# Loading the norm weights inside the first chunk of x, and warming the matrix engine with 44 matmuls instead of 28

## The chip, the core and the metric

The kernel runs on one core of a Trainium2 chip. The metric is the device time of one execution in microseconds (us); lower is better. Three executions of the kernel before took 485.05, 485.16 and 486.32 us, so the median is 485.16 us. The engines that appear below are PE (TensorE: matmuls; PEld is its weight loading), DVE (VectorE), ACT (ScalarE), POOL (GpSimd) and SP, whose queue issues the kernel's DMAs.

## What is computed

A decoder layer with two attention branches (block-sparse "MoBA" and "NSA") over 512 tokens of width 1024. For the change only the first lines matter:

```python
def rms_norm(x, g):
    xf = x.astype(jnp.float32)
    y = xf * lax.rsqrt(jnp.mean(xf * xf, axis=-1, keepdims=True) + EPS)
    return (y * g.astype(jnp.float32)).astype(x.dtype)
...
h = rms_norm(x, norm_w[l])
proj = h @ w_in[l]
(q_a, k_a, v_a, z_a, q_b, kc, vc, ksl, vsl, kwn, vwn, gate_b, z_b, gate_m) = jnp.split(proj, split_points, axis=-1)
```

`x` is (1, 512, 1024) and `norm_w` has 1024 numbers. After it come the two attentions, their gates, two branch projections, the output projection and the addition of `x`.

## The kernel before, in words

The input is kept channel by token: `xT` is cut into eight chunks of 128 channels by 512 tokens, and chunk k is loaded into the tile `x` number k (one 256 KB DMA each). `norm_w` is laid out as 128 by 8, so that column k holds the weights of chunk k, and is loaded into the tile `w` (4 KB).

Every matmul is done in three parts to keep float32 accuracy: a value is split into a rounded part (`hh` of the input, `wh` of a weight tile) and the rest (`hl`, `wl`). `x_split` (L389) makes `hh` on ACT (L393, x times its weight column) and `hl` on DVE (L394). `x_square` (L400) squares each chunk on ACT (L406) and adds the squares up on DVE (L411) into `sq`. The factor 1/rms is not needed before the first projections: they run on the raw product, and `x_rms` (L425) sums `sq` over the channels with a few small matmuls (`pss`, L430), forms `rx` on DVE (L433) and POOL (L434, a power), and the results are scaled by `rx` when they leave PSUM.

The weights come as a stream of 256 KB tiles `wr`; four raw buffers exist (`NRAW`), so the fifth load waits until the first tile has been split. `wh` is made on ACT (L296) or POOL (L298), `wl` on DVE or POOL (L300). Two input chunks share one weight tile.

The first projection, `v0`, is `gemm_first` (L510): for each chunk k it issues twelve matmuls into four accumulators `pgf`, one for each 128 tokens, four with `hh` and `wh`, four with `hl` and `wh`, four with `hh` and `wl` (L523). So it can start as soon as chunk 0 and weight tile 0 have been split. The accumulators are read out (`v`, ACT L607 and DVE L608) once `rx` is known. The second projection, `qk0`, is `gemm_tok` (L497, matmuls at L325): four results `pgt` of 24 matmuls each; the first two use PSUM buffers of another ring, the third and fourth those that `v0` used, so that the third waits for the first `v`. After it come `pR` and `prx` (L627, L460), the next projections, and the transposes `pq` (L777) of the attention.

Before the first real matmul the kernel runs `NWARM` small matmuls of 128 columns on a zero tile (L386), which nobody reads.

The order of the instructions on every engine is worked out while the kernel is built: a planner keeps an estimated time for every engine and for the DMA queue (`dma`, L211, adds at least 450 ns for a load), and emits each step when its inputs should be ready. A change of one estimate thus can change the order elsewhere.

Of the kernel before, what the change touches and what calls it, by code (L numbers as in the profile page):

```python
# [12 lines left out]
F32 = mybir.dt.float32  # L13
F32R = mybir.dt.float32r
AF = mybir.ActivationFunctionType
ALU = mybir.AluOpType
AX = mybir.AxisListType

S = 512
D = 1024  # L20
DH = 64
P = 128
NT = S // P
KT = D // P
# [13 lines left out]
NGM = 5  # L38
NW = 8
NRAW = 4  # L40
NWARM = 28
LAT = 60
SHARE_A = 1.0
SHARE_F = 1.1
# [11 lines left out]
def tok_pieces():  # L56

    r = lambda a, n: list(range(a, a + n))
    d = {f"qk{p}": r(QA + 128 * p, 128) + r(KA_ + 128 * p, 128) for p in range(4)}
    d.update({f"v{i}": r(VA + 256 * i, 256) for i in range(2)})  # L60
    d.update({f"qb{i}": r(QB + 256 * i, 256) for i in range(2)})
    d["kb"] = r(KSL, 128) + r(KWN, 128) + r(GB, 24)
    d["vb"] = r(VSL, 128) + r(VWN, 128)
    return d


def chan_pieces():

    out = {"kc": KC, "vc": VC}
    for j in range(4):  # L70
        out[f"za{j}"] = ZA + 128 * j
        out[f"zb{j}"] = ZB + 128 * j
    for j in range(16):
        out[f"gm{j}"] = GM + 128 * j
    return out


def tok_layout():

    lay, n = {}, 0  # L80
    for name, cols in tok_pieces().items():
        lay[name] = (n, KT // 2, len(cols))
        n += KT // 2
    return lay, n


@with_exitstack
def hybrid_kernel(ctx: ExitStack, tc: tile.TileContext, x, xT, norm_w, wtok, wchan, gains, w1,
                  relone, wbr, wout, consts, out):
    nc = tc.nc  # L90
    cp = ctx.enter_context(tc.tile_pool(name="cp", bufs=1))
# [11 lines left out]
    def nm(s):  # L103
        uid[0] += 1
        return f"{s}{uid[0]}"
# [105 lines left out]
    def dma(dst, src, n, t=None):  # L211

        nc.sync.dma_start(out=dst, in_=src)
        free["Q"] = max(free["Q"], (now[0] if t is None else t) + 1000) + max(450, n * P / 360)
        return free["Q"] + 1000
# [127 lines left out]
    identr = cp.tile([P, P], F32R, name="identr")  # L343
    onesr = cp.tile([P, P], F32R, name="onesr")
    nc.vector.tensor_copy(onesr, ones.to_broadcast([P, P]))
    w8 = cp.tile([P, KT], F32, name="w8")
    rx = cp.tile([P, NT], F32, name="rx")
    nrx = cp.tile([P, NT], F32, name="nrx")
    R = cp.tile([P, S], F32, name="R")
    nc.scalar.activation(R[:, :8], mhalf, AF.Exp)  # L350
    kcs = cp.tile([P, 2, 2, C32], F32R, name="kcs")
    gate = cp.tile([P, 24, NT], F32, name="gate")
    cp.tile([P, 8], F32, name="pad")

    def cview(name):
        o, n = COFF[name]
# [15 lines left out]
    def att(name, dt=F32R):  # L372
        return ap_.tile([P, 512], dt, name=nm(name), tag="a")

    xts = [att("x", F32) for _ in range(KT)]
    xat = {}

    def load_x(k):
        xat[k] = dma(xts[k], xT[k * P:(k + 1) * P, :], 2048)

    now[0] = 700.0
    load_x(0)
    dma(w8, norm_w, 32)
    pw = pg.tile([P, 512], F32, name="pw", tag="g")
    for _ in range(NWARM):
        nc.tensor.matmul(pw[:, :P], warm[:, :1].to_broadcast([P, P]), warm[:, :1].to_broadcast([P, P]), start=True,  # L386
                         stop=True)

    def x_split(k):  # L389

        w = w8[:, k:k + 1]
        c = Chain(xat[k])
        c.do({"A": 613}, lambda e: e.activation(hh[:, k, :], xts[k], AF.Copy, scale=w)).mark(f"xh{k}")  # L393
        c.do({"d": 666}, lambda e: e.scalar_tensor_tensor(hl[:, k, :], xts[k], w, hh[:, k, :].bitcast(F32),  # L394
                                                          op0=ALU.mult, op1=ALU.subtract)).mark(f"xl{k}")

    sq_sum = att("sq", F32)
    sums = Chain(0.0)
# [66 lines left out]
    tlay, _ = tok_layout()  # L465
# [802 lines left out]
    for k in range(1, KT):  # L1268
        if k % 2:
            W.load()  # L1270
        load_x(k)
    W.load()
    W.bufs -= 1
    for k in range(KT):
        x_split(k)
        x_square(k)
# [30 lines left out]
def _consts():  # L1307
    i = np.arange(S)
    edges = np.array([16, 21, 27, 35, 46, 59, 77, 99, 128, 166, 216, 280, 363, 470])
    dist = S - 1 - i  # L1310
    bucket = np.where(dist < 16, dist, 16 + (dist[:, None] >= edges[None, 1:]).sum(1))
    onehot = (np.arange(32)[:, None] == bucket[None, :]).astype(np.float32)
    ident = np.eye(P, dtype=np.float32)
    ii = np.concatenate([np.eye(64, dtype=np.float32)] * 2, 0)
    t = np.arange(NT)[None, :] * P + np.arange(P)[:, None]
    c = np.arange(C32)
    cmask = np.where(16 * c[None, None, :] + 31 <= t[:, :, None], 0.0, NEG).astype(np.float32)
    rowv = (t >= 31).astype(np.float32)
    hmask = (np.arange(P)[:, None] // 64 == np.arange(2)[None, :]).astype(np.float32)
    return onehot, dict(ident=ident, ii=ii, cmask=cmask.reshape(P, -1), rowv=rowv, hmask=hmask)  # L1320


def _layout(inp):
    f = {k: np.asarray(v) for k, v in inp.items()}
    w_in = f["w_in"][0]
    lay, n = tok_layout()
    wtok = np.zeros((n, P, WT), np.float32)
    for name, cols in tok_pieces().items():
        i0, nt, m = lay[name]
        wtok[i0:i0 + nt, :, :2 * m] = w_in[:, cols].reshape(nt, 2, P, m).transpose(0, 2, 1, 3).reshape(nt, P, 2 * m)  # L1330
    ch = lambda w: w.reshape(-1, 4, P, P).transpose(0, 2, 1, 3).reshape(-1, P, 4 * P)
    wchan = np.stack([ch(w_in[:, c:c + P]) for c in chan_pieces().values()])
    gains = np.concatenate([f[k][0] for k in ("q_norm_a", "k_norm_a", "q_norm_b", "k_norm_cmp",
                                               "k_norm_sel", "k_norm_win")])
    posT = np.stack([f[k][0].reshape(16, 2, DH).transpose(1, 2, 0).reshape(P, 16)
                     for k in ("cmp_pos_k", "cmp_pos_v")], 1)
    w1 = np.stack([f[k][0].reshape(8, 2, P, CMPH).transpose(0, 2, 1, 3).reshape(8, P, 512)
                   for k in ("cmp_w1_k", "cmp_w1_v")])
    w2 = np.stack([f[k][0].reshape(2, P, DH).transpose(1, 0, 2) for k in ("cmp_w2_k", "cmp_w2_v")], 1)
    wbr = np.stack([np.concatenate([ch(f[k][0][:, j * P:(j + 1) * P]) for k in ("w_branch_a", "w_branch_b")], 0)  # L1340
                    for j in range(8)])
    wo = f["w_out"][0].reshape(4, 2, P, 4, 256).transpose(3, 0, 2, 1, 4).reshape(4, 4, P, 512)
    onehot, cd = _consts()
    cd.update(pos=posT.reshape(P, -1), w2=w2.reshape(P, -1))
    d = dict(x=f["x"][0], xT=f["x"][0].T, norm_w=f["norm_w"][0].reshape(KT, P).T, wtok=wtok, wchan=wchan, gains=gains, w1=w1,
             relone=np.tile(np.concatenate([f["rel_bias"], onehot], 1), (2, 1)), wbr=wbr, wout=wo,
             consts=np.concatenate([cd[k] for k in COFF], 1))
    return {k: np.ascontiguousarray(v) for k, v in d.items()}


_ORDER = ["x", "xT", "norm_w", "wtok", "wchan", "gains", "w1", "relone", "wbr", "wout", "consts"]


# [16 lines left out]
```

## Time and profile before

| | us |
|---|---|
| median of three executions | 485.16 |
| the profiled execution | 486.89 |
| its span, first to last instruction | 485.1 |
| PE busy in the span | 475.4 (98%) |
| DVE busy | 338.4 (70%) |
| ACT busy | 256.6 (53%) |
| POOL busy | 159.0 (33%) |

The profiled execution took 1.8 us more than its span, and 1.7 us more than the median of the three others. Times in rows are microseconds from the start of the span. The granted clock is given as a share of full speed; a matmul of 256 columns starts every 0.21 us at the lower of the engine's two clock levels (1.2 GHz) and every 0.12 us at the higher one (2.4 GHz), so that the spacing of matmuls tells the level too. A wait is put down to what ended it last.

### The profile page before, as it was taken

How to read it: one execution, taken by the hardware profiler on the slowest of the kernel's cores; microseconds unless marked ns; L12 is line 12 of the kernel's file. 1: busy time of each engine (PE TensorE's matmuls, PEld its weight loads, DVE VectorE, ACT ScalarE, POOL GpSimd, SP SyncE). 2: the span in 40 equal slices, each digit the busy share in tenths (PEclk: the TensorE clock that was granted, in tenths of full speed). 3: DMA queues.
4: the chain of work that ended last, by engine and by line, in shares of the span. 5: the costliest groups of instructions: out<-in, count | busy, mean ns of one | idle time of the engine just before them, and what ended most of it. 6: DMA issues, size and time to landing. Idle time of an engine off the chain costs nothing.

```text
span 485.1 us, 8685 instructions
## 1 busy us (share of the span) xinstructions
PE 475.4 (98%) x3060; PEld 426.7 (88%) x3060; DVE 338.4 (70%) x862; ACT 256.6 (53%) x631; POOL 159.0 (33%) x211
## 2 busy tenths in 40 slices
PE   7999999999999999999999999998999999999997
PEld 7999899999999989888888888886788888889997
DVE  5888999688898589797788677775555535444331
ACT  7656695477675286766686477764222231222210
POOL 0165577165555025465440254354000000000000
PEclk9999999999999999999999999998999999999999
DMA  8737243544344224122212221211133324526421
GB/s 275 221 74 171 61 134 112 151 114 135 79 123 140 74 66 113 41 65 68 65 45 75 84 68 57 49 42 45 43 106 112 94 81 139 166 76 217 142 89 43
DMA packets 28124, 49.15 MB, mean 101 GB/s; under 512 B 3313, under 2 KB 5745, under 8 KB 28081
## 3 DMA queue, kind: packets, MB, share of 16 engines
q1 hardware_dynamic: 28080, 48.60, 34.8%
q8 instruction: 24, 0.39, 0.4%
q14 instruction: 20, 0.16, 0.1%
HBM read 45.84 MB, written 2.75 MB: 100 GB/s over the span
## 4 chain that ended last, share of the span: by engine, by line
PE 95%; DVE 2%; DMA 1%; issue 0%; ACT 0%; POOL 0%; SPq 0%; DVEq 0%
PE pgc L325 30%; PE pgt L325 21%; PE po L325 9%; PE pbr L325 9%; PE O L926 6%; PE pt L892 6%; PE sps L845 3%; PE sps L846 3%; PE pgf L523 3%; PE pq L777 2%; PE hps L692 1%; DMA wr<-in_wtok 1%; PE hps L691 1%; PE scp L1014 1%; PE O L1070 0%
## 5 line engine op out<-in xcount | busy, mean ns | idle before, releaser
L300 DVE TENSOR_TENSOR wl<-wr,wh 128x512 fp32r<-128x512 f32 (+1 forms) x118 | 83.0, 712 | 7.3 <-ACT wh L296 7.0
L325 PE MATMUL pgc<-hh,wh 128*128 128x512 f32 x208 | 84.5, 406 | 0.0
L325 PE MATMUL pgt<-wh,hh 128*128 128x256 f32 (+1 forms) x288 | 82.6, 287 | 0.3 <-DVE v L608 0.3
L325 PE MATMUL pgc<-hh,wl 128*128 128x512 f32 x208 | 81.9, 394 | 0.0
L325 PE MATMUL pgc<-hl,wh 128*128 128x512 f32 x208 | 81.8, 393 | 0.0
L325 PE MATMUL pgt<-wl,hh 128*128 128x256 f32 (+1 forms) x288 | 81.2, 282 | 0.0
L325 PE MATMUL pgt<-wh,hl 128*128 128x256 f32 (+1 forms) x288 | 81.0, 281 | 0.0
L296 ACT CAST wh<-wr 128x512 fp32r<-128x512 f32 (+1 forms) x90 | 54.0, 616 | 27.5 <-DMA wr<-in_wout 21.9
L883 POOL TENSOR_SCALAR P<-P,sst,gate 128x512 f32<-128x512 f32 (+3 forms) x56 | 40.5, 727 | 62.8 <-DVE sst L882 46.8
L298 POOL TENSOR_SCALAR wh<-wr 128x512 fp32r<-128x512 f32 (+1 forms) x34 | 23.3, 687 | 114.9 <-DMA wr<-in_wchan 70.3
L864 DVE CUSTOM_DVE_ANT_0 sb<-sps,T 128x512 f32<-128x512 f32 (+3 forms) x96 | 46.0, 484 | 17.7 <-PE sps L846 16.6
L325 PEld LDWEIGHTS pgt<-wh,hh 128*128 128x128 f32 x288 | 54.3, 188 | 1.2 <-DVE v L608 0.5
L325 PEld LDWEIGHTS pgt<-wh,hl 128*128 128x128 f32 x288 | 54.2, 188 | 0.3
L325 PEld LDWEIGHTS pgt<-wl,hh 128*128 128x128 f32 x288 | 54.3, 188 | 0.0
L879 ACT ACTIVATE P<-sb,sst 128x512 f32<-128x512 f32 (+3 forms) x88 | 50.9, 580 | 6.3 <-DVE sst L864 6.0
L904 ACT CAST ph<-pt 128x512 fp32r<-128x512 f32 (+2 forms) x72 | 33.5, 477 | 26.0 <-PE pt L892 25.3
L325 PEld LDWEIGHTS pgc<-hl,wh 128*128 128x128 f32 x208 | 39.1, 188 | 9.1
L325 PEld LDWEIGHTS pgc<-hh,wh 128*128 128x128 f32 x208 | 39.1, 188 | 6.8
L325 PEld LDWEIGHTS pgc<-hh,wl 128*128 128x128 f32 x208 | 39.2, 188 | 6.7
L892 PE MATMUL pt<-cst,P 128*128 128x128 f32 x232 | 41.8, 278 | 0.3 <-POOL P L883 0.3
L906 DVE TENSOR_TENSOR pl<-pt,ph 128x512 fp32r<-128x512 f32 (+2 forms) x72 | 38.5, 548 | 4.1 <-ACT ph L904 3.7
L370 POOL TENSOR_TENSOR nr<-nss,mhalf 128x4 f32<-128x4 f32 x28 | 32.3, 1157 | 21.4 <-DVE nss L369 19.4
(208 smaller groups left out, 1076.6 us busy)
## 6 DMA issues: line engine op xcount, KB each, us to landing
wr<-in_wchan SPq DMA_DIRECT2D x52, 256.0 KB, 2.7
wr<-in_wtok SPq DMA_DIRECT2D x36, 256.0 KB, 2.8
T<-rtab SPq DMA_DIRECT2D x16, 256.0 KB, 3.8
wr<-in_w SPq DMA_DIRECT2D x16, 256.0 KB, 2.7
wr<-in_wbr SPq DMA_DIRECT2D x16, 256.0 KB, 2.6
wr<-in_wout SPq DMA_DIRECT2D x16, 256.0 KB, 2.9
x<-in_xT SPq DMA_DIRECT2D x8, 256.0 KB, 5.2
xr<-in_x SPq DMA_DIRECT2D x8, 256.0 KB, 4.4
```

Of the source, the lines that this page charges most:

```text
L296: e.copy(hi, raw)
L298: e.tensor_scalar(hi, raw, 1.0, 1.0, op0=ALU.mult, op1=ALU.mult)
L300: c.do(either(n), lambda e, hi=hi, lo=lo, raw=raw: e.tensor_sub(lo, raw, hi.bitcast(F32))).mark((w, 1, i))
L325: nc.tensor.matmul(dst, sts[i][a], mvs[i][b], start=(start and i == a == b == 0), stop=(stop and i == n - 1 and b == 1))
L370: c.do({"p": 430 + 150 * w}, lambda e: e.tensor_tensor(v(dst), v(ss), mhalf[:parts, :w], op=ALU.pow))
L864: e.tensor_tensor_reduce(z["sb"][:, :L], sps[:, :L], T[:, S - L:], scale=-1.0, scalar=3e38, op0=ALU.add, op1=ALU.min, accum_out=st[:, 0, b ...
L879: e.activation(pv(), z["sb"][:, :L], AF.Exp, bias=st[:, 0, b:b + 1], scale=-1.0, accum_out=st[:, 1, b:b + 1])
L883: c.do({"P": 315 + 0.834 * L}, lambda e: e.tensor_scalar(pv(), pv(), st[:, 2, b:b + 1], g, op0=ALU.mult, op1=ALU.mult))
L892: nc.tensor.transpose(pt[:, (b - kb) * P:(b - kb + 1) * P], u.p0 if u.p0 is not None and b == 0 else u.pb[:, POFF[b] + kb * P:POFF[b] + (k ...
L904: e.copy(z["w"][0], pt[:, :w])
L906: ch.do({"D": cd(w)}, lambda e: e.tensor_sub(z["w"][1], pt[:, :w], z["w"][0].bitcast(F32)), pt)
L926: nc.tensor.matmul(O[0][:, S - n:], v.bitcast(F32) if kb == 3 else v, w, start=(u.first and kb == 0 and i == 0), stop=(u.last and kb == 3 ...
```

## The change

`norm_w` is no longer an input of its own. On the host its 128 by 8 layout is put beside the first chunk of x, as columns 512 to 519 of a new input `x0` of 128 by 520. One DMA of 2080 B in each partition loads both into a tile `first`. That tile is taken from the ring `P` (two buffers, otherwise used by the attention and by `bias_rows`) and is given back when the last `hl` is done. The tile `w`, a 4 KB DMA and its place in SP's queue go away. `NWARM` becomes 44.

```diff
-NWARM = 28
+NWARM = 44
...
-    w8 = cp.tile([P, KT], F32, name="w8")
...
-    cp.tile([P, 8], F32, name="pad")
...
-    xts = [att("x", F32) for _ in range(KT)]
+    first = alloc("P", "x0", (P, 1280))
+    w8 = first[:, S:S + KT]
+    xts = [first[:, :S]] + [att("x", F32) for _ in range(1, KT)]
...
-        xat[k] = dma(xts[k], xT[k * P:(k + 1) * P, :], 2048)
+        xat[k] = dma(xts[k], xT[(k - 1) * P:k * P, :], 2048)
...
-    load_x(0)
-    dma(w8, norm_w, 32)
+    xat[0] = dma(first[:, :S + KT], x0, 2080)
...
                                                           op0=ALU.mult, op1=ALU.subtract)).mark(f"xl{k}")
+             first if k == KT - 1 else None).mark(f"xl{k}")
...
-    d = dict(x=f["x"][0], xT=f["x"][0].T, norm_w=f["norm_w"][0].reshape(KT, P).T, ...
+    d = dict(x=f["x"][0], xT=f["x"][0].T[P:],
+             x0=np.concatenate([f["x"][0].T[:P], f["norm_w"][0].reshape(KT, P).T], 1), ...
```

The planner counts one load less, and so the order changes on every engine from the first microseconds to about the first `pq` and the projections beside it; after that it is the same as before. Three places are shown. On SP, the fifth weight tile is now issued before the constants instead of behind them.

DVE, from the last `hl` to the last addition to `sq`. `sq` is the sum of the squares, `gn` and `relr` are small constants, `wl` are weight tiles, in the order in which `qk0` uses them. Before:

```order
L394 SCALAR_TENSOR_TENSOR hl<-x_113,w_98,hh 128x512
L1174 TENSOR_SCALAR gn<-gn 128x64
L1170 TENSOR_TENSOR relr<-rel,relr 32x16
L411 TENSOR_TENSOR sq_145<-sq_145,xsq_287 128x512
L300 TENSOR_TENSOR wl_206<-wr_195,wh_205 128x512
L1174 TENSOR_SCALAR gn<-gn 128x64
L411 TENSOR_TENSOR sq_145<-sq_145,xsq_324 128x512
L300 TENSOR_TENSOR wl_250<-wr_241,wh_249 128x512
L300 TENSOR_TENSOR wl_291<-wr_279,wh_290 128x512
L411 TENSOR_TENSOR sq_145<-sq_145,xsq_326 128x512
L300 TENSOR_TENSOR wl_330<-wr_317,wh_329 128x512
```

The same place now:

```order
L393 SCALAR_TENSOR_TENSOR hl<-x_111,x_104,hh 128x512
L300 TENSOR_TENSOR wl_219<-wr_202,wh_218 128x512
L1174 TENSOR_SCALAR gn<-gn 128x64
L411 TENSOR_TENSOR sq_158<-sq_158,xsq_300 128x512
L1170 TENSOR_TENSOR relr<-rel,relr 32x16
L300 TENSOR_TENSOR wl_263<-wr_254,wh_262 128x512
L1174 TENSOR_SCALAR gn<-gn 128x64
L300 TENSOR_TENSOR wl_304<-wr_292,wh_303 128x512
L411 TENSOR_TENSOR sq_158<-sq_158,xsq_333 128x512
L300 TENSOR_TENSOR wl_344<-wr_325,wh_343 128x512
L411 TENSOR_TENSOR sq_158<-sq_158,xsq_335 128x512
```

The four weight tiles of `qk0` stand earlier, and the last of them now stands ahead of the last addition to `sq`.

DVE, from `rx` to the read-out of `v0`; `dg` is a diagonal tile for a later step, `v` the read-out of one accumulator `pgf`. Before:

```order
L433 TENSOR_SCALAR rx<-pss_380 128x4
L300 TENSOR_TENSOR wl_409<-wr_364,wh_408 128x512
L443 TENSOR_TENSOR rxl<-rx,rxh 128x4
L608 SCALAR_TENSOR_TENSOR v_417<-pgf_170,rx,v_417 128x4x64
L447 TENSOR_TENSOR dg_391<-cst,rxh 128x512
L608 SCALAR_TENSOR_TENSOR v_418<-pgf_171,rx,v_418 128x4x64
```

The same place now:

```order
L433 TENSOR_SCALAR rx<-pss_407 128x4
L300 TENSOR_TENSOR wl_421<-wr_376,wh_420 128x512
L443 TENSOR_TENSOR rxl<-rx,rxh 128x4
L447 TENSOR_TENSOR dg_414<-cst,rxh 128x512
L608 SCALAR_TENSOR_TENSOR v_437<-pgf_183,rx,v_437 128x4x64
L608 SCALAR_TENSOR_TENSOR v_438<-pgf_184,rx,v_438 128x4x64
```

`dg` now stands ahead of the first `v`.

PE, around the sum over channels `pss`; `pgt_348` (now `pgt_363`) is the first result of `qk0`, `pgt_401` (now `pgt_403`) the second. Before:

```order
L325 MATMUL pgt_348<-wh_290,hl 128x256
L325 MATMUL pgt_348<-wl_291,hh 128x256
L430 MATMUL pss_380<-ones,sq_145 128x1 x4
L325 MATMUL pgt_348<-wh_329,hh 128x256
L325 MATMUL pgt_348<-wh_329,hl 128x256
L325 MATMUL pgt_348<-wl_330,hh 128x256
```

The same place now:

```order
L325 MATMUL pgt_403<-wh_218,hh 128x256
L325 MATMUL pgt_403<-wh_218,hl 128x256
L325 MATMUL pgt_403<-wl_219,hh 128x256
L430 MATMUL pss_407<-ones,sq_158 128x1 x4
L325 MATMUL pgt_403<-wh_218,hh 128x256
L325 MATMUL pgt_403<-wh_218,hl 128x256
```

`pss` stood behind 18 matmuls of `qk0` and stands behind 27 now.

## Rows read from the trace of the kernel before

**Rows 1.** The chain of work that ended last, by engine.

```profile
PE 95%; DVE 2%; DMA 1%; issue 0%; ACT 0%; POOL 0%; SPq 0%; DVEq 0%
```

**Rows 2.** PE's waits: us in total, times, longest.

```profile
PE pgf L523 <- ACT wh L296: 2.3, 1, 2.3
```

**Rows 3.** Timeline of the first 7 us: start, us, engine, operation, idle before.

```profile
0.72 0.39 SPq L213 DMA_DIRECT2D x<-in_xT  x1
0.87 3.17 PE L386 MATMUL pw<-warm 128*128 128x128 bf16 x28 [0.87 <-POOL ones L338]
1.17 0.42 SPq L213 DMA_DIRECT2D w<-in_norm_w  x1
1.64 0.42 SPq L213 DMA_DIRECT2D wr<-in_wtok  x1
3.62 0.72 ACT L393 ACTIVATE hh<-x,w 128x512 fp32r<-128x512 f32 x1 [1.40 <-DMA w<-in_norm_w]
5.69 0.62 ACT L296 CAST wh<-wr 128x512 fp32r<-128x512 f32 x1 [1.34 <-DMA wr<-in_wtok]
6.36 1.22 PE L523 MATMUL pgf<-wh,hh 128*128 128x256 f32 x4 [2.32 <-ACT wh L296]
```

**Rows 4.** Tile x, time from issue to landing; DMA issues with KB and median landing.

```profile
DMA to landing us min/median/max: 2.6/5.2/5.6
wr<-in_wtok SPq DMA_DIRECT2D x36, 256.0 KB, 2.8
w<-in_norm_w SPq DMA_DIRECT2D x1, 4.0 KB, 2.4
```

**Rows 5.** Windows: length, busy us (instructions) of each engine, granted clock, DMA share, GB/s.

```profile
6.40:11.40 5.00, 5.00 (x23) 5.00 (x24) 4.54 (x7) 5.00 (x10) 0.81 (x1) 1.00 1.01 377
```

**Rows 6.** Timeline of PE in the first projection.

```profile
7.38 1.05 PE L523 MATMUL pgf<-wh,hl 128*128 128x256 f32 x4
11.64 0.64 PE L523 MATMUL pgf<-wh,hh 128*128 128x256 f32 x4
```

**Rows 7.** Timeline of PE in the second projection: its start, `pss`, its third result.

```profile
20.19 0.28 PE L325 MATMUL pgt<-wh,hh 128*128 128x256 f32 x1
22.34 0.95 PE L430 MATMUL pss<-ones,sq 128*128 128x1 f32 x8
26.75 0.28 PE L325 MATMUL pgt<-wh,hh 128*128 128x256 f32 x1
```

**Rows 8.** Timeline of DVE and POOL from the second `hl` to the first `v`.

```profile
7.49 1.77 DVE L394 SCALAR_TENSOR_TENSOR hl<-x,w,hh 128x512 fp32r<-128x512 f32 x2 [0.46 <-ACT hh L393]
...
9.78 0.68 DVE L300 TENSOR_TENSOR wl<-wr,wh 128x512 fp32r<-128x512 f32 x1
...
20.27 0.68 DVE L411 TENSOR_TENSOR sq<-sq,xsq 128x512 f32<-128x512 f32 x1
20.87 0.68 DVE L300 TENSOR_TENSOR wl<-wr,wh 128x512 fp32r<-128x512 f32 x1
...
25.54 0.48 DVE L608 SCALAR_TENSOR_TENSOR v<-pgf,rx,v 128x256 fp32r<-128x256 f32 x1
25.71 1.04 POOL L447 TENSOR_TENSOR dg<-cst,rxl 128x512 fp32r<-128x512 f32 x1 [0.28 <-DVE rxl L443]
25.94 1.36 DVE L447 TENSOR_TENSOR dg<-cst,rxh 128x512 fp32r<-128x512 f32 x1
```

**Rows 9.** Timeline of ACT, DVE and PE before the first transposes `pq`.

```profile
39.25 0.47 ACT L560 ACTIVATE nraw<-pgt,rx 128x256 f32<-128x256 f32 x1 [1.72 <-PE pgt L325]
40.05 0.42 DVE L549 TENSOR_TENSOR qk<-nxn,qk 128x256 fp32r<-128x256 f32 x1 [0.24 <-ACT qk L548]
41.16 1.14 PE L777 MATMUL pq<-identr,qk 128*128 128x128 f32 x12
```

**Rows 10.** Windows at the end of the attention; columns as in rows 5.

```profile
328.00:332.00 4.00, 2.70 (x16) 1.76 (x14) 3.49 (x11) 2.66 (x9) 3.09 (x5) 1.00 0.09 26
332.40:335.90 3.50, 3.44 (x12) 2.75 (x13) 1.49 (x3) 1.42 (x4) 1.22 (x3) 0.51 0.24 88
```

More of the change, by code (lines that the diff above doesn't have):

```diff
@@ L87, in hybrid_kernel @@
 @with_exitstack
-def hybrid_kernel(ctx: ExitStack, tc: tile.TileContext, x, xT, norm_w, wtok, wchan, gains, w1,
+def hybrid_kernel(ctx: ExitStack, tc: tile.TileContext, x, x0, xT, wtok, wchan, gains, w1,
                   relone, wbr, wout, consts, out):
@@ L394, in x_split @@
         c.do({"d": 666}, lambda e: e.scalar_tensor_tensor(hl[:, k, :], xts[k], w, hh[:, k, :].bitcast(F32),
-                                                          op0=ALU.mult, op1=ALU.subtract)).mark(f"xl{k}")
+                                                          op0=ALU.mult, op1=ALU.subtract),
+             first if k == KT - 1 else None).mark(f"xl{k}")
     sq_sum = att("sq", F32)
@@ L1344, in _layout @@
     cd.update(pos=posT.reshape(P, -1), w2=w2.reshape(P, -1))
-    d = dict(x=f["x"][0], xT=f["x"][0].T, norm_w=f["norm_w"][0].reshape(KT, P).T, wtok=wtok, wchan=wchan, gains=gains, w1=w1,
+    d = dict(x=f["x"][0], xT=f["x"][0].T[P:],
+             x0=np.concatenate([f["x"][0].T[:P], f["norm_w"][0].reshape(KT, P).T], 1), wtok=wtok, wchan=wchan, gains=gains, w1=w1,
              relone=np.tile(np.concatenate([f["rel_bias"], onehot], 1), (2, 1)), wbr=wbr, wout=wo,
@@ L1348, in _layout @@
     return {k: np.ascontiguousarray(v) for k, v in d.items()}
-_ORDER = ["x", "xT", "norm_w", "wtok", "wchan", "gains", "w1", "relone", "wbr", "wout", "consts"]
+_ORDER = ["x", "x0", "xT", "wtok", "wchan", "gains", "w1", "relone", "wbr", "wout", "consts"]
 def kernel(**inputs):
```

## The prediction

> **What bounds the kernel now.** I read the chain of waits first: PE carries 95% of it [rows 1], so the time is PE's work plus the stretches in which PE stands still or runs slowly. PE's waits come next: the longest by far is the one before the first real matmul, 2.3 us for the first split weight tile [rows 2]. The timeline of the first 7 us shows what leads there. The 28 warming matmuls run from 0.87 to 4.04; the first weight tile, issued third at 1.64, lands and is split at 5.69; PE starts at 6.36 [rows 3]. The norm weights hold up only the first hh, at 3.62, which is done 1.3 us before ACT gets its weight tile: on the path they are not a wait but 4 KB and a place in the queue.
>
> The window behind the start shows a second loss. Its granted clock reads 1.00, but the matmuls say otherwise: between the group at 7.38 and the one at 11.64 lie 20 matmuls, one each 0.213 us, which is 256 columns at 1.2 GHz; from 11.64 to 20.19 there are 72, one each 0.119 us, the 2.4 GHz level [rows 5 to 7]. Before the slow stretch PE had stood for 2.32 us [rows 3]. The first 24 matmuls took 11.64 - 6.36 = 5.28 us; at the higher level they take 24 x 0.119 = 2.86. So 2.4 us lie in the clock there.
>
> Last I read what PE would meet if it came earlier: DVE, which works without a wait from 7.49 to the last addition to sq at 20.95 [rows 8], while PE reached pss only at 22.34 [rows 7].
>
> **The change part by part.**
>
> The load of norm_w: SP issues everything behind it up to 0.47 us earlier (1.17 against 1.64) [rows 3]. The transfers themselves still queue behind the first chunk, which lands at 0.72 + 2.6 = 3.3, while w landed at 1.17 + 2.4 = 3.6 [rows 3, 4]. I take that difference, 0.25 us, for the first weight tile and all that follows; the bounds are 0 and 0.47. There is one larger bound: this tile took 4.0 us (1.64 to 5.69) where the median is 2.8 [rows 3, 4]. If the small transfer is what held it up, it lands at about 1.17 + 2.8 to 3.2, some 1.2 us earlier than now. I keep that as a rival.
>
> The first chunk has rows of 2080 B instead of 2048, 1.6% more; of a transfer that fills 2.6 us at most this is under 0.05 us and I count nothing. A rule speaks against the layout: the Trainium skill's page "DMA: Bandwidth & Descriptors", section "How a descriptor splits into AXI transactions", says that a read that does not start on a 256-byte boundary fetches bytes that it does not use, and rows of 2080 B mostly start off it. As an estimate from that page, up to a tenth of one chunk's transfer, under 0.1 us; by it the gain below would be 0.9 instead of 1.0. No run here shows it yet.
>
> The 16 more warming matmuls: 28 take 3.17 us with a last one of 0.31, so one each 0.106; 44 end at 0.87 + 43 x 0.106 + 0.31 = 5.74 at the low clock. PE would start at 6.36 - 0.25 = 6.1. They lie wholly in the 2.32 us of idle time [rows 3] and cost nothing, unless the weight tile comes more than 0.35 us earlier still; then each further tenth is lost to them.
>
> The clock: PE then pauses for 0.4 us instead of 2.3 before the real work, after 4.9 us of matmuls instead of 3.2. I take it that the higher level is there when the real work starts or at once after: gain 2.4 us. Bounds: 0 (the rise comes where it came) and 2.4.
>
> What is late next. With 2.4 + 0.25 us gained, PE would end gemm_first at 17.5. It must wait about 0.3 us for the second wl, done at 10.46 - 0.25 [rows 8], and 0.3 to 0.4 for the fourth wl of qk0. The weight tiles of qk0 stand earlier on DVE now, else it would be more. So PE is at pss, behind 27 matmuls, at 17.5 + 0.7 + 27 x 0.119 = 21.4, not at 22.34.
>
> The sum in sq is late in the same way. DVE has the same work up to its last addition, plus the one wl that now stands ahead of it, 0.60 us (20.27 to 20.87) [rows 8]: 20.95 - 0.25 + 0.60 = 21.3. So pss starts at 21.4 by either, 0.94 us earlier than before. From there everything hangs on rx: in the trace the first v is done at 25.54 + 0.48 = 26.02, 3.68 us behind the start of pss, and the third result of qk0 needs its buffer; PE started that at 26.75 without a wait [rows 7, 8]. Now dg stands ahead of that v. Before, DVE's dg took 1.36 us, and it started 0.23 us after POOL's dg, which ended at 26.75; from there it needed only 0.55 [rows 8]. Now DVE's comes first, because POOL's needs rxl from DVE. I price it at 0.60, the spacing of the other 512-column operations of two tiles; the upper bound is 1.36. The first v is done at 21.4 + 3.68 + 0.60 = 25.7.
>
> That DVE's dg was waiting and not merely slow is what the Trainium skill states ("SBUF — State Buffer", section "Who interferes with whom"): a DVE operation with two inputs in SBUF and a GpSimd operation that reads SBUF exclude each other, and the first one holds the ports. The two rows agree. Without that rule one would take 1.36 and the third result would start at 26.5.
>
> So the third result starts at about 25.75 instead of 26.75, although PE itself would be there at 21.4 + 0.95 + 21 x 0.119 = 24.85 [rows 7]: a new wait of about 0.9 us for v. The gain that is left is 1.0 us.
>
> Behind it: PE meets the first pq with 15 fewer matmuls ahead, 1.8 us sooner by plan: 25.75 + 14.4 - 1.8 = 38.4, where 14.4 is 41.16 - 26.75. Its last input was done at 40.47 [rows 9]. One microsecond earlier that is 39.5, and PE would wait 1.1 us. But in the trace the ACT step ahead of it stood behind a read-out that waited for PE until 39.25 [rows 9]; in the new order it stands before that read-out, and the multiplication by the gains goes from POOL to DVE. I count no wait (bounds 0 and 1.1). The matmuls themselves are the same, and from there on the order is too, so the 1.0 us should stay to the end. The tile in ring P is given back when the last hl is done, before gemm_first ends, and nothing asks for a second buffer there sooner: no cost.
>
> Sum: -0.25 (queue) - 2.4 (clock) + 0.7 (weight splits) + 0.9 to 1.0 (wait for v) = about -1.0 us. The profiled execution would go from 486.89 to 485.9; its median stood 1.7 us lower, at 485.16, and so I predict 484.2 us.
>
> **The rivals.**
>
> 1. The front of the chain moves as well: the first weight tile lands 1 us earlier still, because the small transfer had held it up. For it speaks its 4.0 us against a median of 2.8 [rows 3, 4]; against it, that the other first loads are slow too (5.2 us for the chunks of x), for they share the bandwidth. DVE then starts up to 1 us earlier and the gain is about 2.0 us: 483.1.
>
> 2. Almost no gain: the clock does not rise sooner, or dg keeps its 1.36 us, or pq waits its 1.1 us. By the second, v is done at 26.45 and the gain is 0.3; by the third it is 0 to 0.1; by the first, PE is at pss no earlier than 22.34 - 0.25, and behind it stands dg: 22.1 + 3.68 + 0.60 = 26.4, gain 0.4. All end at 484.7 to 485.2.
>
> 3. Slower: the new wait before the third result drops the clock. At the end of the attention PE was busy for 2.70 of 4.00 us, and then the granted clock was 0.51 for 3.5 us [rows 10], worth some 1.7 us. If v comes at 26.45 or later, while PE arrives at 24.85, there are 1.6 us of idle time close behind the 0.7 us for the weight splits; from there the low level can follow, and 0.3 gained turns into 1.4 lost: 486.6. Against it: with 1 us of idle time the stretch is much fuller than that one, and a wait like it is less than half the 2.3 us at the start.
>
> **How the numbers follow.** Forecast (gain 0.5 to 1.4) 48%, rival 1 (1.4 to 2.6) 27%, rival 2 (0 to 0.5) 17%, rival 3 8%. The clock of an execution moves the start by some tenths in either direction, and the three runs of before already differ by 1.3 us. What this measurement can tell from no change is 0.3%, 1.46 us. The forecast lies inside that: same. Faster takes nearly all of rival 1 and the tail of the forecast, 0.30; slower is rival 3, 0.07; same 0.63. The range reaches over rivals 1 and 2 to 482.6 and 485.7; it leaves out rival 3 and the last part of rival 1.
>
> **What would show it.** The timeline of the changed kernel: warming matmuls until about 5.7 or less, the first weight split at about 5.4, the first real matmul at 6.1 with a spacing of 0.119 us soon after; pss at 21.4; DVE's dg of 0.6 to 0.7 us, then the first v; a wait of PE for v of about 0.9 us, in place of the 2.3 us for wh; the third result at 25.75 and pq at 38.4 without a wait. I am wrong if PE does not wait for v (then the gain is larger), if the matmuls behind 6.1 keep 0.213 us for long, or if PE waits for the last input of pq.

## The result: slower, and the profile after

The changed kernel takes 488.87 us (median of 12 executions, 487.40 to 492.63); the kernel before, beside it, 486.15 us (12 executions, 485.05 to 487.58). The ratio is 1.0061, 95% interval 1.0039 to 1.0083. So the change makes the kernel slower by 2.7 us. I had forecast 484.2 us, with 486.6 for the slow rival; "slower" had a chance of 0.07. The profiled execution took 488.03 us (span 486.2), 1.1 us more than the one of before (486.89). That pair shows less than the medians; a second profile, below, closes the gap.

The front does more than I had forecast. Timeline of the changed kernel, first 9 us (columns as in [rows 3]):

```profile
0.87 4.83 PE L385 MATMUL pw<-warm 128*128 128x128 bf16 x44 [0.87 <-POOL ones L338]
1.17 0.42 SPq L213 DMA_DIRECT2D wr<-in_wtok  x1
...
3.44 0.72 ACT L392 ACTIVATE hh<-x 128x512 fp32r<-128x512 f32 x1 [1.22 <-DMA x<-in_x]
...
4.13 0.62 ACT L296 CAST wh<-wr 128x512 fp32r<-128x512 f32 x1
...
5.51 0.89 PE L523 MATMUL pgf<-wh,hh 128*128 128x256 f32 x4
...
8.60 0.63 PE L523 MATMUL pgf<-wh,hh 128*128 128x256 f32 x4
```

The first weight tile is split at 4.13 instead of 5.69 [rows 3]. PE goes from the last warming matmul into the first real one without a wait, and 24 matmuls take 8.60 - 5.51 = 3.09 us where they took 5.28 [rows 3, 6]. At the second projection PE and DVE read:

```profile
20.88 0.95 PE L430 MATMUL pss<-ones,sq 128*128 128x1 f32 x8
...
24.08 0.68 DVE L447 TENSOR_TENSOR dg<-cst,rxh 128x512 fp32r<-128x512 f32 x1
24.25 1.42 POOL L447 TENSOR_TENSOR dg<-cst,rxl 128x512 fp32r<-128x512 f32 x1 [0.28 <-DVE rxl L443]
24.68 1.66 DVE L608 SCALAR_TENSOR_TENSOR v<-pgf,rx,v 128x256 fp32r<-128x256 f32 x4
25.31 0.36 PE L325 MATMUL pgt<-wh,hh 128*128 128x256 f32 x1 [0.92 <-DVE v L608]
```

The third result of `qk0` starts at 25.31 instead of 26.75 [rows 7]: 1.44 us are gained there. They don't last. PE's waits in the changed kernel (columns as in [rows 2]):

```profile
PE pq L777 <- DVE qk L549: 2.5, 2, 2.1
...
PE pgt L325 <- DVE v L608: 1.1, 2, 0.9
```

PE's wait of 2.3 us for `wh` [rows 2] is gone, the wait for `v` is there as forecast, and at the top stands one that before did not have: `pq` for `qk`. Its longest piece, 2.1 us, lies 29 us behind the wait for `v`. Compared matmul by matmul, the two profiles share one order of 2724 matmuls from 45.51 us of before to the end. The changed kernel is 0.71 us ahead on the matmul before that `pq`, 1.52 us behind on it, and 1.26 us behind on the last one of the kernel. What decides the result is this one stall of 2.23 us.

The chain of waits of the changed kernel from 20 to 56 us leads from there to its cause (start, us, what):

```profile
33.80 0.61 DVE rt L631
...
34.47 7.74 DMA rtab<-rt
42.23 4.28 DMA T<-rtab
...
46.66 0.19 DVE sb L864
...
47.36 0.33 DVE nss L570
...
48.85 1.03 POOL nr L368
...
51.30 1.03 POOL nr L368
...
53.68 0.41 ACT qk L548
54.12 0.42 DVE qk L549
```

`rt` holds the relative bias of 16 heads; `bias_rows` writes it to memory sixteen times over (`rtab`, 640 KB), and each head then loads its tile `T` from there with shifted rows. `sb` is the first step on a head's scores and needs `T`. `nss`, `nr`, `nxn` and `qk` are the norm steps of a result of `qk1`, whose `qk` the transposes `pq` wait for. `sb` has nothing to do with them, but DVE works in order. Timeline of DVE, and of that `pq`, in the changed kernel:

```profile
44.13 0.43 DVE L567 TENSOR_TENSOR nxn<-nxn,gn 128x256 f32<-128x256 f32 x1
46.66 0.69 DVE L864 CUSTOM_DVE_ANT_0 sb<-sps,T 128x512 f32<-128x512 f32 x1 [2.10 <-DMA T<-rtab]
...
47.27 0.41 DVE L570 TENSOR_REDUCE nss<-nxn 128x4 f32<-128x256 f32 x1
...
54.12 0.42 DVE L549 TENSOR_TENSOR qk<-nxn,qk 128x256 fp32r<-128x256 f32 x1 [0.47 <-ACT qk L548]
...
54.60 0.28 PE L777 MATMUL pq<-identr,qk 128*128 128x128 f32 x1 [2.12 <-DVE qk L549]
```

And the kernel before in the same place, SP's two issues and DVE:

```profile
33.95 0.33 SPq L213 DMA_DIRECT2D rtab<-rt  x1
41.81 1.23 SPq L213 DMA_DIRECT2D T<-rtab  x2
...
44.30 2.11 DVE L784 CAST kx<-pq 64x512 fp32r<-64x512 f32 x3
46.44 1.19 DVE L300 TENSOR_TENSOR wl<-wr,wh 128x512 fp32r<-128x512 f32 x1
47.56 0.41 DVE L570 TENSOR_REDUCE nss<-nxn 128x4 f32<-128x256 f32 x1
47.89 0.68 DVE L864 CUSTOM_DVE_ANT_0 sb<-sps,T 128x512 f32<-128x512 f32 x1
```

There `sb` stood behind casts of `pq`, weight splits and the first `nss`, and came to its turn at 47.89, when `T` had landed. The table was as late there (33.95 against 34.47), but nobody noticed. In the new order some of the casts are on ACT, DVE is at `sb` at 44.56, and `nss` stands behind it.

### The profile page after: what moved, and what is told of

Read it like the earlier page. It is cut to its first block, busy times and chain, and to the rows that moved or that the text cites. A ratio compares the mean times of both kernels' runs of the same rounds, so it can differ in the third digit from the quotient of the medians.

```text
span 486.2 us, 8718 instructions
## 1 busy us (share of the span) xinstructions
PE 475.8 (98%) x3076; PEld 426.6 (88%) x3076; DVE 337.2 (69%) x862; ACT 257.9 (53%) x632; POOL 159.5 (33%) x210
## 4 chain that ended last, share of the span: by engine, by line
PE 81%; DVE 9%; DMA 5%; issue 2%; POOL 1%; ACT 1%; SPq 1%; POOLq 0%; DVEq 0%
PE pgc L325 28%; PE pgt L325 14%; PE po L325 9%; PE pbr L325 9%; PE O L926 6%; PE pt L892 5%; PE sps L845 3%; PE sps L846 3%; DMA rtab<-rt 2%; DVE wl L300 1%; PE pq L777 1%; DMA x<-in_xT 1%; POOL nr L368 1%; DMA oh<-in_relone 1%; DMA T<-rtab 1%
```

## The experiments

The theory, T: the loss is the table's lateness met by `sb`'s new place ahead of the norm steps in DVE's queue, and not the merged load or the warming themselves. Rivals: the longer warming costs the time (W); the time is lost to the new order in many places; the merged load is worth nothing by itself. Timed runs have 4 to 12 executions. They were taken in three series (e1 to e4, e5 to e8, e9 and e10), each beside 17 or 29 executions of the kernel before, whose medians lie between 485.59 and 485.85. A ratio compares within a series, so versions of different series are compared by their ratios.

**e1: the changed kernel with 28 warming matmuls**, same order.

```diff
-NWARM = 44
+NWARM = 28
```

> The changed kernel with 28 warming matmuls again; the order of every engine is that of the changed kernel. Theory T (the loss is DVE standing for the bias table T in front of the norm steps that pq needs, by the new order and the late table): the first projection runs at the lower clock again for some 5 us, but the bias table lands no sooner, at 46 to 47.5 us, the step sb still waits for it, and pq behind it; time 487.5 to 489.5 us, about that of the changed kernel, not that of before. Rival W (the 16 more warming matmuls cost the time, by themselves or through the clock): the time falls back to that of before, 485.5 to 486.5 us.

Measured: 489.64 us, ratio 1.0082 [1.0055, 1.0110], no faster. The stall stays:

```profile
47.23 0.69 DVE L864 CUSTOM_DVE_ANT_0 sb<-sps,T 128x512 f32<-128x512 f32 x1 [2.17 <-DMA T<-rtab]
...
55.18 0.28 PE L777 MATMUL pq<-identr,qk 128*128 128x128 f32 x1 [2.21 <-DVE qk L549]
```

The stall is as long with 28 matmuls as with 44, so W falls.

**e2: the kernel before with 44 warming matmuls**, same order as before.

```diff
-NWARM = 28
+NWARM = 44
```

> The kernel before with 44 warming matmuls and nothing else; its order is kept. Theory T: the first projection ends up to 2 us earlier, the sum of squares and rx hold the third result of qk0 at about 26, sb stands further back in DVE's order and waits under 0.5 us for the table; pq waits under 1 us; time 484.5 to 486, ratio 0.996 to 1.000. Rival W (warming matmuls cost): 487.5 to 489 us.

Measured: 485.86 us, ratio 1.0000 [0.9987, 1.0013]. In its profile the real matmuls run at the higher level from the second one on:

```profile
0.88 4.87 PE L386 MATMUL pw<-warm 128*128 128x128 bf16 x44 [0.88 <-POOL ones L338]
5.89 0.74 PE L523 MATMUL pgf<-wh,hh 128*128 128x256 f32 x4
...
8.86 0.63 PE L523 MATMUL pgf<-wh,hh 128*128 128x256 f32 x4
```

24 matmuls in 2.97 us. PE is 2.8 us ahead at 11.64 us of before. Of this, 0.46 is not the clock's: the first weight tile was split at 5.22 in this execution, though its load is that of before. By 21 us PE has stood four times around `qk0` for weight splits (0.37 to 0.62 us from one matmul to the next, instead of 0.12), and 0.44 us are left. So the warming alone is worth nothing that the medians show: DVE is late next, as the prediction said.

**e3: the changed kernel with the bias table ahead of `qk0`.**

```diff
-        yield from proj_norm("qk0", 0, "ttgg")
         yield from bias_rows()
+        yield from proj_norm("qk0", 0, "ttgg")
```

> The changed kernel with the bias rows (pR, rt, the write of rtab) put ahead of qk0 instead of behind it: they need only the constants. Theory T: rtab is issued at about 22 to 25 us instead of 34.5, the table T is there before sb is reached, the 2.1 us wait of sb for T is gone and with it the 2.5 us of waits of PE for qk; time 485 to 486.7 us, 2 to 3 us less than the changed kernel. Rival O (the new order of the norm steps alone delays qk, the table has nothing to do with it): pq still waits over 1.5 us and the time stays at 488 or more.

Measured: 484.38 us, ratio 0.9973 [0.9957, 0.9990]. The table is issued at 20.64 and neither `sb` nor `pq` waits:

```profile
45.08 0.68 DVE L864 CUSTOM_DVE_ANT_0 sb<-sps,T 128x512 f32<-128x512 f32 x1
```

It fits T, but the edit moves many other steps too, so that alone it shows little.

**e4: the planner told what the table takes** (nothing else; it counts 3.8 us from issue to landing, the trace 7.74).

```diff
-            done["rtab"] = dma(rtab...
+            done["rtab"] = 4000 + dma(rtab...
```

> The changed kernel, where the planner is told that the bias table's write ends 4 us later than it thought, nearer to the 7.7 us seen in the trace: nothing runs differently but the order behind it (T's load, sps and sb later, norm steps ahead of them). Theory T: sb no longer holds DVE in front of the norm steps, its wait is under 0.7 us, pq waits under 0.7 us; time 485 to 487 us. Rival O: pq still waits over 1.5 us and the time stays at 488 or more.

Measured: 485.59 us, ratio 0.9997 [0.9984, 1.0010]. `rtab` is issued at 34.8, as late as ever, but the planner now puts `sb` behind more of the norm steps:

```profile
46.97 0.69 DVE L864 CUSTOM_DVE_ANT_0 sb<-sps,T 128x512 f32<-128x512 f32 x1
```

`sb` does not wait, and by the ratios (1.0061 and 0.9997) 3.1 us are back. A late table under another order does no harm.

**e5: the same engine order, the table in two parts.** 80 KB for heads 0 and 1 are written first and the whole table when their `T` are loaded.

```diff
+            nc.sync.dma_start(out=rtab0..., in_=rt[:2]...)
...
-        row = rtab[0, h:h + 1, :]
+        row = (rtab0 if h < 2 else rtab)[0, h:h + 1, :]
...
+        if h == 1:
+            whole.pop()()
```

> The changed kernel with every engine's order kept, but the bias table's write is cut in two: a small one with the rows of the first two heads (80 KB instead of 640 KB), from which T of these heads is loaded, and the whole table only behind these loads. Theory T: the small write lands some 3 to 5 us after its issue instead of 7.7, T is there before sb is reached, sb's wait of 2.1 us for T falls under 0.5 and the waits of PE for qk before pq from 2.5 to under 0.8 us; time 485.5 to 487 us against 488.9 of the changed kernel. Rival O (the order of the norm steps alone holds qk back): the waits of PE for qk stay over 1.5 us and the time at 488 or more.

Measured: 486.11 us, ratio 1.0013 [1.0002, 1.0024]. Timeline of SP and DVE:

```profile
34.43 0.30 SPq L636 DMA_DIRECT2D rtab<-rt  x1
38.79 1.24 SPq L213 DMA_DIRECT2D T<-rtab  x2
...
44.43 0.68 DVE L872 CUSTOM_DVE_ANT_0 sb<-sps,T 128x512 f32<-128x512 f32 x1
```

The small write is issued at the same time, and `T`, which needs it, can be issued 4.4 us later instead of 7.8. `sb` runs without a wait. Up to that `pq` the kernel is level with the changed one, within 0.1 us; from it on it is 2.23 us ahead, just what the changed one had lost there. By the ratios the edit gives back 2.3 us. An early table under the harmful order does no harm either. e4 and e5 together are T: it takes both.

**e6: the changed kernel in the order of before.** The planner is charged the 438 ns of the load that went away, and then emits on every engine the order of before.

```diff
     xat[0] = dma(first[:, :S + KT], x0, 2080)
+    free["Q"] += 438.4
```

> The changed kernel (norm weights in the first load, 44 warming matmuls), with the 0.44 us that the planner no longer counts put back into its estimate of the DMA queue: every engine then has the order of the kernel before. Theory T: sb stands behind the norm steps as before, does not wait for T by more than 0.3 us, pq does not wait for qk; some of the front's gain is lost to the weight splits of qk0; time 484.5 to 486 us, ratio 0.996 to 1.000. Rival M (merging the load or warming longer costs by itself): 487.5 us or more.

Measured: 484.30 us, ratio 0.9976 [0.9965, 0.9986]. In the first 60 us PE waits for none of `wh`, `v` and `qk`, and DVE not for `T`. PE's longest waits that are left:

```profile
PE O L927 <- DVE pl L907: 1.5, 4, 0.6
PE pw L386 <- POOL ones L338: 0.9, 1, 0.9
PE pbr L325 <- ACT yh L967: 0.7, 1, 0.7
```

The table is issued 1.9 us earlier than in before (32.10), because what computes it is earlier.

**e7: e3 with 28 warming matmuls.**

> The changed kernel with the bias rows ahead of qk0, and 28 warming matmuls. The table is out of the way, so the clock can show what it is worth. Theory T: the first projection has 8 to 24 slow matmuls again, 0.8 to 2.3 us, of which the 1.6 us wait for v takes up most: 0.3 to 1.0 us slower than with 44 (484.4), 484.7 to 485.4 us. Rival C (the clock at the start carries through to the end): 486 us or more.

Measured: 485.50 us, ratio 1.0001 [0.9985, 1.0017], 0.1 us above what I had expected. Against e3 the 16 matmuls are worth 1.1 us by the medians and 1.4 by the ratios, whose intervals just overlap. The profile does not show why. I had expected 8 to 24 slow matmuls, and only the first one is slow; from the second on they are 0.12 us apart:

```profile
4.80 0.75 PE L523 MATMUL pgf<-wh,hh 128*128 128x256 f32 x4 [0.75 <-ACT wh L296]
5.38 0.64 PE L523 MATMUL pgf<-wh,hl 128*128 128x256 f32 x4
```

**e8: the kernel before with the table ahead of `qk0`** (the edit of e3 without the change).

> The kernel before with the bias rows ahead of qk0 and nothing else: the control of the third experiment. Theory T: in the kernel before nobody waited for the table, so putting it earlier gives little, 0 to 0.7 us: 485.2 to 486.2 us. Rival E (the early bias rows are worth 1.5 us or more by themselves, whatever the change did): 484.4 us or less.

Measured: 500.60 us, ratio 1.0316 [1.0299, 1.0332]. A miss by both theories. The edit made the planner order the whole program anew. PE's waits now lie in many places:

```profile
PE O L926 <- DVE pl L906: 3.3, 6, 1.2
PE pgf L523 <- ACT wh L296: 2.0, 1, 2.0
PE pgt L325 <- POOL wl L300: 2.0, 1, 2.0
```

I did not follow them further. It says nothing on the table (issued at 20.06), but shows what an edit by way of the planner can do, and takes from e3 its worth as proof.

Its start bears on the warming. PE ran 28 warming matmuls and then stood for 1.98 us, and yet its real matmuls are at the higher level from the second one on; the next group of four starts at 6.59:

```profile
6.02 0.74 PE L523 MATMUL pgf<-wh,hh 128*128 128x256 f32 x4 [1.98 <-ACT wh L296]
```

**e9: e6 with 28 warming matmuls**, the merged load alone in the order of before.

> The merged load with 28 warming matmuls and exactly the order of the kernel before: beside the version with 44 (484.30 us) and the kernel before with 44 (485.86 us) this fills the last corner of merge by warming. If the merge alone is worth something once the order stays (theory M): first weight split at 4.1 as in the other versions with the merged load, first real matmul at 4.8 at the low level, spacing of 0.119 us from about 9.4, about 1.2 us before the kernel before at that point and still 0.5 to 1.2 us at the end: 485.0 to 485.7 us. If both parts are needed together, because the matmuls then start early and at the higher level (theory B): no gain that can be told, 485.8 to 486.4 us. Theory T on the table: no wait for T and none for qk, by either.

Measured: 484.69 us, ratio 0.9979 [0.9966, 0.9992], 0.3 us better than the best that I had expected of M. Timeline of PE:

```profile
0.87 3.17 PE L386 MATMUL pw<-warm 128*128 128x128 bf16 x28 [0.87 <-POOL ones L338]
4.78 1.22 PE L524 MATMUL pgf<-wh,hh 128*128 128x256 f32 x4 [0.74 <-ACT wh L296]
5.80 1.05 PE L524 MATMUL pgf<-wh,hl 128*128 128x256 f32 x4
...
9.98 0.63 PE L524 MATMUL pgf<-wh,hh 128*128 128x256 f32 x4
```

M holds: the merged load gains by itself, though the first 23 matmuls run at the lower level.

**e10: the changed kernel once more**, for a second profile.

> The changed kernel once more, for a second profile. The wait of sb for T is a matter of the order and of the table's 7.7 us, so it should stand in every execution (theory T): sb waits 1.8 to 2.4 us, and the pq behind it 2 to 2.6 us. If the timed runs lose more than the profiled one because the low clock level comes more often, the granted clock in the windows behind 50 us shows a second dip in an execution of 489 us or more; if this one takes about 488 us, one dip or none.

Measured: 489.23 us.

```profile
47.73 0.69 DVE L864 CUSTOM_DVE_ANT_0 sb<-sps,T 128x512 f32<-128x512 f32 x1 [2.39 <-DMA T<-rtab]
...
55.68 0.28 PE L777 MATMUL pq<-identr,qk 128*128 128x128 f32 x1 [2.30 <-DVE qk L549]
```

The stall is there again. The rest was a miss: I had looked for a second dip of the clock behind 50 us, and there is one dip, as in the profile of before (0.83 in the window from 330 to 340 us in both). Instead the first matmuls run at the lower level a little longer, 0.75 us by the tenth microsecond, and the stall is 0.3 us longer. Against the profile of before it is 2.60 us behind at that `pq` and 2.46 at the end, near the 2.7 of the medians.

The four timed versions in the order of before and the two in the new one, with the edits apart (median us; ratio to the kernel before of the same series):

| | 28 warming matmuls | 44 warming matmuls |
|---|---|---|
| `norm_w` apart, order of before | 485.83, reference | 485.86, 1.0000 |
| merged, order of before | 484.69, 0.9979 | 484.30, 0.9976 |
| merged, new order | 489.64, 1.0082 | 488.87, 1.0061 |

By the ratios the merged load is worth 1.0 us, the warming behind it 0.1 more, which cannot be told from nothing, and the order that comes with the change costs 5.0 us with 28 matmuls and 4.1 with 44. The fastest versions that ran are e3 and e6, which their ratios don't tell apart; e6 has all of the change but its order.

## Why the prediction was wrong, step by step

The load: under-sized. I took 0.25 us with bounds 0 and 0.47, and kept 1.2 as the mechanism of the first rival. The split came 1.56 us earlier. Part of that is the one profile of before that I had: with `norm_w` apart the tile was split at 5.69, in e2 at 5.22 and in e8 at 5.35; with the merged load it was split between 4.09 and 4.44. So the gain is 0.8 to 1.6 us, and what happened is what the first rival says. SP's queue accounts for 0.47 of it. The rest lies between issue and landing: 3.6 to 4.0 us in before, e2 and e8, 2.9 in the changed kernel and 3.2 in e10. That the 4 KB transfer ahead of the tile is the reason was not tried by itself.

Rows of 2080 B: right, nothing to see. The chunk landed 2.7 us after its issue in the changed kernel and 3.1 in e10, where it took 2.6 in before [rows 4] and 2.7 in e2. The estimate that I drew from the Trainium skill ("DMA: Bandwidth & Descriptors", section "How a descriptor splits into AXI transactions") was under 0.1 us, and the traces can neither bear it out nor refute it.

The 16 warming matmuls: the case that I named came in. The tile was ready at 4.75, PE still had warming to do until 5.51, and 0.7 us of the earlier tile were lost to it, as e9 shows with 4.78. The clock made up for it: 24 matmuls took 3.09 us, a gain of 2.2 where I had 2.4. But the profiles don't show that the 16 matmuls brought this gain. With 44, the first 1 to 6 real matmuls were slow in all seven profiles. With 28, it was 21 to 24 in three (before, e1, e9), and only the first in two (e7, e8), in e8 behind a standstill of 1.98 us. So the slow start that I read in the trace of before is not there in every execution, and to take all of it for the gain of the change was luck in part. What the warming is worth stands in the medians: 0.0 us (e2), and 0.1 to 1.4 with the merged load.

The weight splits cost 0.7 us, as priced, and `pss` starts at 20.88 where I had 21.4. `dg`: 24.68 - 24.08 = 0.60 us, as priced, and POOL's `dg`, now the later one, takes 1.42 instead of 1.04 [rows 8]. These rows agree with the rule of the Trainium skill ("SBUF — State Buffer", section "Who interferes with whom"): whoever comes second waits. The wait for `v`: 0.92 where I had 0.9, and the third result at 25.31 where I had 25.75. So up to the third result the sum held, with half a microsecond to spare: the load gave 1.3 us more than its term, and 0.7 was lost to the warming and 0.2 in the clock. The slow rival's mechanism did not come in: between 20 and 60 us the granted clock is 1.00, and the matmuls keep the spacing of the higher level behind both waits (0.12 us for 256 columns, 0.23 for 512).

The step that failed is the last one before the sum: "I count no wait (bounds 0 and 1.1)" for the first `pq`, and "from there on the order is too, so the 1.0 us should stay to the end". The first `pq` did wait, for a last input that came late by 0.6 us, within the bounds; of 1.44 us gained, 0.71 are left on the common order. The second is what turned the gain into a loss: instead of staying, it was lost to a stall of 2.23 us at a later `pq`. That the order is the same behind about the first `pq`, as the section on the change says, holds for PE, from 45 us on; DVE's differs up to 54 us, and I had compared the order around the terms of my sum and not all of it up to the end of the difference. Neither `T` nor `sb` has a term in the sum. I asked what PE meets if it comes earlier, but of DVE only as far as `v`. The question that was missing is the same one a step further: DVE comes earlier to a step whose input does not move. That input was to be read from the trace of before, where `T` was issued only at 41.81.

The profile of e6 shows where the order costs time. Matmul by matmul, the changed kernel is 0.64 us ahead of it at 23 us, 0.51 behind at 30 (the wait for `v`), 1.19 behind at 45 (the first `pq`) and some 3.4 behind from the stall on, up to 328 us. A dip of the clock makes it 3.8: from 333.2 to 336.7 us the granted clock is 0.51 in the changed kernel's profile, and e6's has no dip. So the 3.9 us between the two profiles are accounted for. Of the 4.1 us that the ratios give for the order, the stall is a little more than half (2.2 in the first profile, 2.4 in e10), and e5 gave it back; the wait for `v` and the first `pq` were not undone one by one.

## What to carry to other kernels

Where a planner writes the order, the smallest edit of a load is also an edit of the order, and the order may be worth more than the edit: here 4 to 5 us against about 1. So compare the order on every engine up to where the difference ends, and for each engine that now comes earlier look up the landing of every load that it meets there. Then time the edit in the old order as well, which a single charge in the planner's account brought back.

## What the runs showed of the hardware that was not expected

The write of the table, 640 KB from 16 partitions, takes 7.7 us from issue to landing in the changed kernel, and 8.4 in e5. Behind a write of 80 KB from two partitions the next load could be issued after 4.4 us (e5). Eight times less data saves less than half. DMAs of the changed kernel (KB, median us from issue to landing):

```profile
T<-rtab SPq DMA_DIRECT2D x16, 256.0 KB, 3.8
rtab<-rt SPq DMA_DIRECT2D x1, 640.0 KB, 7.7
```

A 4 KB load ahead of the first weight tile goes with a split of that tile 0.8 to 1.6 us later (5.22 to 5.69 against 4.09 to 4.44), though its place in SP's queue is worth 0.47.

The level of the clock at the start differs from one execution to the next: with 28 warming matmuls the first 24 real ones took 5.28 us in before, and in e7 and e8 all but the first ran at the higher level.
